# Interleaving two arrays: loads with 63 KiB reads over two SBUF rows

## The chip, the cores and the metric

The kernel runs on one core of a Trainium2 chip. The metric is the device time of one execution in microseconds (us). Before the change the median of three runs is 314.57 us (314.43 to 314.57).

## The reference

```python
def reference(x, y):                       # both (32, 256, 1024) float32
    batch, seq, dim = x.shape
    result = np.zeros((batch, seq, dim * 2), dtype=np.float32)
    result[..., 0::2] = x
    result[..., 1::2] = y
    return result.astype(np.float32)
```

Each input holds 33.55 MB and the output 67.11 MB. No value is changed; elements of x go to the even places of the output and elements of y to the odd ones. Since the last axis is doubled, the whole is also the interleaving of two flat arrays of 8,388,608 elements, and that is how the kernel treats it.

## The kernel before

**Tiles.** The flat arrays are cut into n = 8 tiles of 128 x 8192 elements (W = 8192). A tile's row, one SBUF partition, is 32 KiB and is contiguous in DRAM, and neighbouring partitions hold neighbouring rows of DRAM. There are two buffers each for x (`xt`), y (`yt`) and the woven output (`ot`); `ot` also has 8192 columns, which is the output of half a tile (H = 4096 columns of x and of y). Each half is called a piece here: piece 2k + h is half h of tile k, and it uses `ot[h]`.

**The engines.** Three of them work, and the order of each is written out by hand, with semaphores between them.

- SyncE (SP) issues the loads: the first half of x0 (line 38), then for each tile k x (line 47) and y (line 50). From tile 2 on, x_k waits until the second x copy of tile k-2 is done (line 45), and y_k until the second y copy is (line 49); the semaphore `woven` counts copies. The queue that these loads run on is q1 in the profile.
- VectorE (DVE) weaves: for each piece a copy of x into the even columns of `ot` (line 62) and a copy of y into the odd ones (line 65). It waits for x and y of the tile at its first piece (lines 57 and 64), and before each x copy for the store that last used this `ot` buffer (line 61).
- ScalarE (ACT) issues a small copy from DRAM to DRAM (line 40), the second half of x0 (line 41), and then a store for each piece as soon as its y copy is done (lines 70 to 73). Its queue is q10 in the profile.

**Descriptors.** In a load or store one row of one partition is one descriptor of the DMA engines: 32 KiB for all but the two halves of x0, which have 16 KiB. The 128 rows are shared out over 16 DMA engines, eight for each. A DMA that completes writes a semaphore once on each engine; these are the packets of 4 bytes in the profile's count.

**Start and end.** `tile_interleave_kernel` moves the first DMA of SyncE and of ScalarE ahead of the opening barrier. At the end ScalarE waits for the stores of `ot[0]` and clears semaphores, and SyncE waits for the stores of `ot[1]` (line 79).

Of the kernel before, what the change touches and what calls it, by code (L numbers as in the profile page):

```python
# [3 lines left out]


def _interleave(nc, x, y, out):
    P = 128
    W = 8192
    H = W // 2  # L10

    total = 1
    for s in x.shape:
        total *= s
    n = total // (P * W)
    assert n * P * W == total

    def rows(ap, names, k):
        flat = ap.rearrange("b s d -> (b s d)")
        return flat[k * names : (k + 1) * names].rearrange("(p w) -> p w", p=P)  # L20

    fp32 = mybir.dt.float32
    xt = [nc.alloc_sbuf_tensor(f"xt{b}", [P, W], fp32).ap() for b in (0, 1)]
    yt = [nc.alloc_sbuf_tensor(f"yt{b}", [P, W], fp32).ap() for b in (0, 1)]
    ot = [nc.alloc_sbuf_tensor(f"ot{b}", [P, W], fp32).ap() for b in (0, 1)]

    xsem = [nc.alloc_semaphore(f"xsem{b}") for b in (0, 1)]
    hsem = nc.alloc_semaphore("hsem")
    tsem = nc.alloc_semaphore("tsem")
    ysem = [nc.alloc_semaphore(f"ysem{b}") for b in (0, 1)]  # L30
    woven = nc.alloc_semaphore("woven")
    osem = [nc.alloc_semaphore(f"osem{b}") for b in (0, 1)]

    xs = [rows(x, P * W, k) for k in range(n)]
    ys = [rows(y, P * W, k) for k in range(n)]
    os_ = [rows(out, 2 * P * W, k) for k in range(n)]

    nc.sync.dma_start(out=xt[0][:, :H], in_=xs[0][:, :H]).then_inc(xsem[0], 16)
    few = (slice(0, P, P // 16), slice(0, 128))
    nc.scalar.dma_start(out=os_[0][few], in_=xs[0][few]).then_inc(tsem, 16)  # L40
    nc.scalar.dma_start(out=xt[0][:, H:], in_=xs[0][:, H:]).then_inc(hsem, 16)
    for k in range(n):
        b = k % 2
        if k >= 2:
            nc.sync.wait_ge(woven, 4 * (k - 2) + 3)
        if k:
            nc.sync.dma_start(out=xt[b], in_=xs[k]).then_inc(xsem[b], 16)
        if k >= 2:
            nc.sync.wait_ge(woven, 4 * (k - 2) + 4)
        nc.sync.dma_start(out=yt[b], in_=ys[k]).then_inc(ysem[b], 16)  # L50

    for k in range(n):
        b = k % 2
        for h in (0, 1):
            c = slice(h * H, (h + 1) * H)
            if h == 0:
                nc.vector.wait_ge(xsem[b], 16 * (k // 2 + 1))
            elif k == 0:
                nc.vector.wait_ge(hsem, 16)
            if k:  # L60
                nc.vector.wait_ge(osem[h], 16 * k)
            nc.vector.tensor_copy(out=ot[h][:, 0::2], in_=xt[b][:, c]).then_inc(woven, 1)  # L62
            if h == 0:
                nc.vector.wait_ge(ysem[b], 16 * (k // 2 + 1))
            nc.vector.tensor_copy(out=ot[h][:, 1::2], in_=yt[b][:, c]).then_inc(woven, 1)  # L65

    nc.scalar.wait_ge(tsem, 16)
    for k in range(n):
        for h in (0, 1):
            nc.scalar.wait_ge(woven, 4 * k + 2 * h + 2)  # L70
            nc.scalar.dma_start(
                out=os_[k][:, h * W : (h + 1) * W], in_=ot[h]
            ).then_inc(osem[h], 16)

    nc.scalar.wait_ge(osem[0], 16 * n)
    used = sorted(s.num for s in [*xsem, hsem, tsem, *ysem, woven, osem[0]])
    assert used == list(range(used[0], used[-1] + 1)), used
    nc.scalar.sem_clear(range(used[0], used[-1] + 1))
    nc.sync.nop(nofuse=True).wait_op(osem[1], 16 * n, "sem-ge").then_inc(
        osem[1], -16 * n  # L80
    )


def kernel(tc, x, y, out):
    nc = tc.nc
    tc.close()
    tc.compile()

    _interleave(nc, x, y, out)

    blocks = nc.main_func.blocks
    for engine in (mybir.EngineType.SP, mybir.EngineType.Activation):
        opening = blocks[0].instructions
        at, moved = next(
            (b, i)
            for b in blocks[1:]
            for i in b.instructions
            if i.engine == engine and i.opcode == "DMACopy"
        )
        assert not (moved.sync_info and moved.sync_info.on_wait)  # L100
        body = at.instructions
        body.remove(moved)
        gate = next(
            n
            for n, i in enumerate(opening)
            if i.engine == engine and i.opcode == "Drain"
        )
        opening.insert(gate, moved)
        at.instructions = body
        blocks[0].instructions = opening  # L110


# [1 line left out]
_INS = ['x', 'y']  # L114
_OUTS = [((32, 256, 2048), 'float32')]


# [23 lines left out]
```

## Time and profile before

| what | value |
|---|---|
| median of three runs | 314.57 us |
| span of the profiled execution, first to last instruction | 313.0 us |
| VectorE busy | 72.6 us, 32 copies |
| DMA packets, bytes, mean pace | 4784, 134.23 MB, 429 GB/s |
| q10 (ScalarE's queue): share of 16 engines' span | 51.2% |
| q1 (SyncE's queue): share of 16 engines' span | 48.5% |
| store, issue to landing, median | 29.1 us |
| y load, issue to landing, median | 60.9 us |

The page gives the span of the profiled execution, and no other time of that execution; the median of the timed runs stands 1.57 us above it. Busy shares are taken over the span. The line called DMA cuts the span into 40 slices, and each digit is the mean busy share of the 16 DMA engines in tenths (9 is 90% or more); in a view cut to a window, the slices are those of the window. A line of a queue gives its packets, the megabytes they moved, and the time they took as a share of what 16 engines have in the span. Beside these views the trace holds a record of each DMA packet (queue, size, start and duration); times of single packets in this document come from there. Within one engine a packet starts as soon as the one before it is through, so the records can be strung together by their times, engine by engine.

A line of the timeline gives start and duration in us, the engine, the line of the kernel, the operation with what it writes and reads, and, in brackets, how long the engine was idle before it and what ended that.

### The profile page before, as it was taken

To read this page: it belongs to the slowest core of one execution; us is meant where nothing else is said; L and a number is where in the kernel's file an instruction comes from. 1 tells how busy PE (TensorE), PEld (TensorE's weight loads), DVE (VectorE), ACT (ScalarE), POOL (GpSimd) and SP (SyncE) were. 2 spreads that over 40 slices of the span, in tenths; PEclk is the share of its full clock that TensorE was granted. 3 is DMA by queue.
4 is the path that set the end of the run, shared out by engine and by line. 5 is a ranking of instruction groups with operands and counts; after the bars stand their busy time and mean duration, and the time that the engine had idled before them with its cause. 6 is when DMAs were issued, how large, how long until landed. Compare 5 with 4: busy or idle time off the path is not lost.

```text
span 313.0 us, 115 instructions
## 1 busy us (share of the span) xinstructions
DVE 72.6 (23%) x32; POOL 0.2 (0%) x4
## 2 busy tenths in 40 slices
DVE  0216002231022410325003250031501305013510
POOL 0000000000000000000000000000000000000000
DMA  8999999999999999999999999999999999999998
GB/s 336 435 435 402 465 406 452 419 448 423 435 435 419 452 402 469 402 469 402 465 406 452 419 448 423 435 435 419 452 402 469 402 469 402 465 406 452 419 448 356
DMA packets 4784, 134.23 MB, mean 429 GB/s; under 512 B 544, under 2 KB 560, under 8 KB 560
## 3 DMA queue, kind: packets, MB, share of 16 engines
q10 hardware_dynamic: 2480, 69.22, 51.2%
q1 hardware_dynamic: 2304, 65.01, 48.5%
HBM read 67.12 MB, written 67.12 MB: 429 GB/s over the span
## 4 chain that ended last, share of the span: by engine, by line
DMA 82%; DVE 12%; issue 0%
DMA out_dram<-ot 76%; DVE ot L65 6%; DMA yt<-in_y_dram 6%; DVE ot L62 6%
## 5 line engine op out<-in xcount | busy, mean ns | idle before, releaser
L62 DVE COPY ot<-xt 128x4096 f32<-128x4096 f32 x16 | 36.7, 2295 | 180.2 <-DMA out_dram<-ot 171.5
L65 DVE COPY ot<-yt 128x4096 f32<-128x4096 f32 x16 | 36.7, 2292 | 45.4 <-DMA yt<-in_y_dram 45.4
L125 POOL MEMSET const-bfloat16-1.0<- 128x1 bf16 x1 | 0.1, 101 | 0.0
L125 POOL MEMSET const-uint8-127<- 128x1 uint8 x1 | 0.1, 101 | 0.0
L125 POOL MEMSET const-float32-1.0<- 128x1 f32 x1 | 0.1, 99 | 0.0
L125 POOL MEMSET const-float32-0.0<- 128x1 f32 x1 | 0.1, 98 | 0.2 <-issue 0.2
## 6 DMA issues: line engine op xcount, KB each, us to landing
out_dram<-ot ACTq DMA_DIRECT2D x16, 4096.0 KB, 29.1
yt<-in_y_dram SPq DMA_DIRECT2D x8, 4096.0 KB, 60.9
xt<-in_x_dram SPq DMA_DIRECT2D x7, 4096.0 KB, 43.7
xt<-in_x_dram SPq DMA_DIRECT2D x1, 2048.0 KB, 8.7
xt<-in_x_dram ACTq DMA_DIRECT2D x1, 2048.0 KB, 17.5
out_dram<-in_x_dram ACTq DMA_DIRECT2D x1, 8.0 KB, 6.1
```

The lines of the kernel that those rows point to most:

```text
L62: nc.vector.tensor_copy(out=ot[h][:, 0::2], in_=xt[b][:, c]).then_inc(woven, 1)
L65: nc.vector.tensor_copy(out=ot[h][:, 1::2], in_=yt[b][:, c]).then_inc(woven, 1)
L125: nc = _bacc.Bacc("TRN2", target_bir_lowering=False, num_devices=1)
```

## The change

W becomes 8064, so that a row has 31.5 KiB and two rows have 63 KiB. The 65,536 columns of a partition are then eight tiles of 8064 and a ninth of 1024. Loads, except the two halves of x0, are issued by a new function `load`: the DRAM side is viewed with `fold` neighbouring rows as one (2 for the eight large tiles, 4 for the ninth), the SBUF side stays a tile of 128 rows. A folded load of a large tile so reads 64 pieces of 63 KiB and writes 128 rows of 31.5 KiB; a load of the ninth reads 32 pieces of 16 KiB and writes 128 rows of 4 KiB. The instruction is built by hand from the two access patterns, as the two shapes differ.

The pieces are now a list. The eight large tiles have two pieces of 4032 columns each, the ninth is a single piece of 1024, so there are 17 pieces and 17 stores (16 with rows of 31.5 KiB, one with rows of 8 KiB). Piece i uses `ot[i % 2]`. The waits keep their meaning and are renumbered to the list; the two semaphores of `ot` change their parts in the closing waits, since the last piece now uses `ot[0]`.

```diff
-    W = 8192
-    H = W // 2
+    W = 8064
+    FOLD = 2
...
+    widths = [W] * (cols // W)
+    if cols % W:
+        widths.append(cols % W)
+    n = len(widths)
...
+    pieces = []
+    for k, w in enumerate(widths):
+        step = w // 2 if w > W // 2 else w
+        pieces += [(k, c, c + step) for c in range(0, w, step)]
...
+    def load(tile, ap, k, sem):
+        w = widths[k]
+        fold = FOLD if w == W else 4
+        wide = rows(ap, k).rearrange("(q r) w -> q (r w)", r=fold)
+        return nc.sync.add_instruction(
+            mybir.InstDMACopy(
+                name=nc.get_next_instruction_name(),
+                mode="Copy",
+                engine=mybir.EngineType.SP,
+                queue="qSPDynamicHW",
+                ins=nc.sync.lower_ap_dma(wide),
+                outs=nc.sync.lower_ap_dma(tile[:, :w]),
+            )
+        ).then_inc(sem, 16)
...
         if k >= 2:
-            nc.sync.wait_ge(woven, 4 * (k - 2) + 3)
+            nc.sync.wait_ge(woven, 2 * last[k - 2] + 1)
         if k:
-            nc.sync.dma_start(out=xt[b], in_=xs[k]).then_inc(xsem[b], 16)
+            load(xt[b], fx, k, xsem[b])
         if k >= 2:
-            nc.sync.wait_ge(woven, 4 * (k - 2) + 4)
-        nc.sync.dma_start(out=yt[b], in_=ys[k]).then_inc(ysem[b], 16)
+            nc.sync.wait_ge(woven, 2 * last[k - 2] + 2)
+        load(yt[b], fy, k, ysem[b])
...
+    for i, (k, a, e) in enumerate(pieces):
         b = k % 2
...
+        if i >= 2:
+            nc.vector.wait_ge(osem[i % 2], 16 * (i // 2))
+        o = ot[i % 2][:, : 2 * (e - a)]
+        nc.vector.tensor_copy(out=o[:, 0::2], in_=xt[b][:, a:e]).then_inc(woven, 1)
+        if a == 0:
+            nc.vector.wait_ge(ysem[b], 16 * (k // 2 + 1))
+        nc.vector.tensor_copy(out=o[:, 1::2], in_=yt[b][:, a:e]).then_inc(woven, 1)
...
+    for i, (k, a, e) in enumerate(pieces):
+        nc.scalar.wait_ge(woven, 2 * i + 2)
+        nc.scalar.dma_start(
+            out=rows(fo, k, 2)[:, 2 * a : 2 * e], in_=ot[i % 2][:, : 2 * (e - a)]
+        ).then_inc(osem[i % 2], 16)
...
-    nc.scalar.wait_ge(osem[0], 16 * n)
+    nc.scalar.wait_ge(osem[1 - end], 16 * (m // 2))
...
```

More of the change, by code (lines that the diff above doesn't have):

```diff
@@ L8, in _interleave @@
     P = 128
-    W = 8192
-    H = W // 2
+    W = 8064
+    FOLD = 2
+    fp32 = mybir.dt.float32
     total = 1
@@ L31, in _interleave @@
     woven = nc.alloc_semaphore("woven")
[L32 to L38, printed above, removed]
+    pieces = []
+    for k, w in enumerate(widths):
+        step = w // 2 if w > W // 2 else w
+        pieces += [(k, c, c + step) for c in range(0, w, step)]
+    last = {}
+    for i, (k, _, _) in enumerate(pieces):
+        last[k] = i
+    m = len(pieces)
+    end = (m - 1) % 2
+    osem = [None, None]
+    for b in (1 - end, end):
+        osem[b] = nc.alloc_semaphore(f"osem{b}")
+    def load(tile, ap, k, sem):
[12 more added lines that the diff above has]
+        ).then_inc(sem, 16)
+    H = widths[0] // 2
+    x0 = rows(fx, 0)
+    nc.sync.dma_start(out=xt[0][:, :H], in_=x0[:, :H]).then_inc(xsem[0], 16)
     few = (slice(0, P, P // 16), slice(0, 128))
-    nc.scalar.dma_start(out=os_[0][few], in_=xs[0][few]).then_inc(tsem, 16)
-    nc.scalar.dma_start(out=xt[0][:, H:], in_=xs[0][:, H:]).then_inc(hsem, 16)
+    nc.scalar.dma_start(out=rows(fo, 0, 2)[few], in_=x0[few]).then_inc(tsem, 16)
+    nc.scalar.dma_start(out=xt[0][:, H : widths[0]], in_=x0[:, H:]).then_inc(hsem, 16)
     for k in range(n):
@@ L44, in _interleave @@
         if k >= 2:
-            nc.sync.wait_ge(woven, 4 * (k - 2) + 3)
+            nc.sync.wait_ge(woven, 2 * last[k - 2] + 1)
         if k:
-            nc.sync.dma_start(out=xt[b], in_=xs[k]).then_inc(xsem[b], 16)
+            load(xt[b], fx, k, xsem[b])
         if k >= 2:
-            nc.sync.wait_ge(woven, 4 * (k - 2) + 4)
-        nc.sync.dma_start(out=yt[b], in_=ys[k]).then_inc(ysem[b], 16)
-    for k in range(n):
+            nc.sync.wait_ge(woven, 2 * last[k - 2] + 2)
+        load(yt[b], fy, k, ysem[b])
@@ L53, in _interleave @@
+    for i, (k, a, e) in enumerate(pieces):
         b = k % 2
[L54 to L65, printed above, removed]
@@ L67, in _interleave @@
-    nc.scalar.wait_ge(tsem, 16)
[L68 to L73, printed above, removed]
-    nc.scalar.wait_ge(osem[0], 16 * n)
-    used = sorted(s.num for s in [*xsem, hsem, tsem, *ysem, woven, osem[0]])
+        if a == 0:
+            nc.vector.wait_ge(xsem[b], 16 * (k // 2 + 1))
+        elif k == 0:
+            nc.vector.wait_ge(hsem, 16)
@@ new lines, in _interleave @@
+        if i >= 2:
+            nc.vector.wait_ge(osem[i % 2], 16 * (i // 2))
+        o = ot[i % 2][:, : 2 * (e - a)]
+        nc.vector.tensor_copy(out=o[:, 0::2], in_=xt[b][:, a:e]).then_inc(woven, 1)
+        if a == 0:
+            nc.vector.wait_ge(ysem[b], 16 * (k // 2 + 1))
+        nc.vector.tensor_copy(out=o[:, 1::2], in_=yt[b][:, a:e]).then_inc(woven, 1)
+    nc.scalar.wait_ge(tsem, 16)
+    for i, (k, a, e) in enumerate(pieces):
[3 more added lines that the diff above has]
+        ).then_inc(osem[i % 2], 16)
@@ L77, in _interleave @@
+    nc.scalar.wait_ge(osem[1 - end], 16 * (m // 2))
+    used = sorted(s.num for s in [*xsem, hsem, tsem, *ysem, woven, osem[1 - end]])
     assert used == list(range(used[0], used[-1] + 1)), used
     nc.scalar.sem_clear(range(used[0], used[-1] + 1))
-    nc.sync.nop(nofuse=True).wait_op(osem[1], 16 * n, "sem-ge").then_inc(
-        osem[1], -16 * n
+    turns = (m + 1) // 2
+    nc.sync.nop(nofuse=True).wait_op(osem[end], 16 * turns, "sem-ge").then_inc(
+        osem[end], -16 * turns
     )
```

15 lines of the change are left out of this document (9 added, 6 removed).

## The prediction

> **What bounds the kernel now.** I read the page's busy shares and slices first, then the DMA queues, the DMA view cut to the steady stretch, the waits of the queue that issues loads, and last the order of time at the start and the end.
>
> ```profile
> span 313.0 us, 115 instructions
> DVE 72.6 (23%) x32; POOL 0.2 (0%) x4
> DMA  8999999999999999999999999999999999999998
> DMA packets 4784, 134.23 MB, mean 429 GB/s; under 512 B 544, under 2 KB 560, under 8 KB 560
> q10 hardware_dynamic: 2480, 69.22, 51.2%
> q1 hardware_dynamic: 2304, 65.01, 48.5%
> ```
>
> VectorE works 23% of the span; the 16 DMA engines work 99.7% of it (51.2 + 48.5). q1 is the queue that SyncE issues on (all loads but one), q10 that of ScalarE (all stores, and half of the first load). So the DMA engines bound the kernel, and only three things can move its end: fewer bytes (there are none to save), less cost per descriptor, or stretches in which the engines stall.
>
> ```profile
> DMA  9999999999999999999999999999999999999999
> DMA packets 3661, 106.86 MB, mean 434 GB/s; under 512 B 400, under 2 KB 400, under 8 KB 400
> q1 hardware_dynamic: 1824, 53.48, 50.3%
> q10 hardware_dynamic: 1837, 53.38, 50.3%
> ```
>
> This is the same view from 40 to 286 us. Both queues are always filled and move the same bytes: in the packet records the engines alternate strictly, one load descriptor, one store descriptor. That turns go by descriptor and not by byte is seen before 18 us, where q1 has 32 KiB and q10 has 16 KiB pieces: there too they alternate one to one.
>
> ```profile
> SPq L47 <- DVE ot L62: 208.4, 6, 40.5
> SPq L50 <- DVE ot L65: 11.1, 6, 1.9
> ```
>
> SyncE's queue waits 208.4 us for a copy to free xt. That costs nothing now, because q1 always has about a load in hand: y2 lands at 93.6 us, x3 was issued at 69.64.
>
> ```profile
> 24.24 2.29 DVE L62 COPY ot<-xt 128x4096 f32<-128x4096 f32 x1
> 24.41 274.16 ACTq L71 DMA_DIRECT2D out_dram<-ot  x16
> 26.44 2.29 DVE L65 COPY ot<-yt 128x4096 f32<-128x4096 f32 x1
> ...
> 293.70 2.30 DVE L62 COPY ot<-xt 128x4096 f32<-128x4096 f32 x1 [3.80 <-DMA out_dram<-ot]
> 295.91 2.29 DVE L65 COPY ot<-yt 128x4096 f32<-128x4096 f32 x1
> ```
>
> The first store is issued at 24.41, the last at 298.2 us, while the store ahead of it runs until 302.9: no gap at the end. The one visible stall is at the first store. The load packets that begin at 27.3 to 27.7 us take 1.61 to 1.89 us where all later ones take 1.213, and the first store packets begin at 29.05; with two packets at 26.1 that is 8.8 us over 16 engines, 0.55 us each.
>
> **Prices of descriptors.** From the packet records, start to start on one engine: 1209.5 ns for 32 KiB, 607 for 16 KiB, 23.5 for 512 B, 6 for a semaphore write. Two sizes give the line: (1209.5 - 607)/16384 = 0.036773 ns per byte, and 607 - 602.5 = 4.5 ns for each descriptor (the 512 B one: 18.8 + 4.7, so the line holds). Before, for each engine: 248 x 1209.5 + 16 x 607 + 34 x 6 + 23.5 = 309.9 us. The first packet begins at 1.0, the engines' slow first packets and the stall add 1.7, the last completion falls at 313.0.
>
> **The change, part by part.** Per engine, with the line above.
>
> Stores: 16 x 8 of 31.5 KiB (1190.7 ns) and 8 of 8 KiB (305.7) = 154.86 us, against 128 x 1209.5 = 154.82. More descriptors, +0.04.
>
> First load in two halves of 15.75 KiB: 16 x 597.6 = 9.56, against 9.71 (fewer bytes, which the ninth tile carries).
>
> The 15 folded loads: 60 reads of 63 KiB and 120 writes of 31.5 KiB. No row of before has a read that is split over two writes. If the 4.5 ns go with the read, one costs 2376.8 ns: 142.61 us. If with the write, it costs 2 x 1190.7: 142.88. The ninth tile's two loads: 4 reads of 16 KiB, 2.43, or 16 writes of 4 KiB, 2.48. Before: 120 x 1209.5 = 145.14.
>
> Semaphore writes: 37 instead of 34, +0.02.
>
> Sum: 309.70 us if the read pays, 310.03 if the write pays: -0.20 or +0.13 us. I take -0.20, as the load and the store of 32 KiB cost the same 1209.5 although one writes to SBUF and the other to DRAM, which fits a cost per transfer that the read opens; but that is weak, and +0.13 stays in the range. [...]
>
> VectorE: 34 copies for 32, sixteen pairs of 4032 columns (4032/4096 x 2.29 = 2.25 us) and one of 1024 (0.57). Each pair, 4.5 us, lies under the other buffer's store, which takes 8 x 1.19 = 9.5 us even with the engines to itself. Without that cover each pair would cost up to 4.5 us. The last small pair, 1.1 us, lies under store 15 in the same way. Costed at nothing.
>
> Waits: the counts of woven are renumbered, the order is the same: x of tile k behind the last x copy of tile k-2, y behind the last y copy. Tile 8's loads stand on SyncE behind the copies of piece 13, with two whole stores still to come, and nothing is queued behind them but the closing wait. On ScalarE store 16 stands last, behind store 15. The two longer waits at the end only swap the two semaphores.
>
> Start: y0 now takes 2.38 us turns against 0.60 of the first load's second half. Counting turns from 8.8 us (three of its eight are done): y0 is through at 20.6 instead of 21.5, the half's completion falls at 23.6 instead of 19.1. So the first y copy may begin some 0.9 us earlier and the second x copy about as before. q1 holds x1 and y1 meanwhile, so the engines stay busy and none of this reaches the end.
>
> Turns: if a turn is a read descriptor, q1 gets 63 KiB to q10's 31.5. A tile's loads (8 reads) then take 8 x (2.38 + 1.19) = 28.5 us of a period of some 38, and q1 stands empty for the other 9 or 10, once before each of tiles 3 to 8: six restarts (x2 and y2 still queue up behind y1). With q1 empty, two stores are in hand at 9.5 us each against 4.5 us of copies, so no engine runs out of work. What a restart costs no row shows. The nearest are two of another queue: q10 began again at 6.36 us with a load of 16 KiB pieces beside q1's and cost nothing (neighbours stayed 611 ns), and began again at 29 us with a store, 0.55 us. Mine are loads, so I take nothing, and keep 6 x 0.55 = 3.3 us as the upper end. The first store's own stall I leave at 0.55; it may vanish.
>
> Forecast on the profiled execution: span 313.0 - 0.2 = 312.8. The page gives no time of that execution around its span; the median of the runs lies 1.57 us above it. So 314.57 - 0.2 = 314.4.
>
> **The rivals.** A measurement of this kernel can tell about 0.2% (0.63 us) from no change.
>
> 1. Restarts cost. Place: q1 when SyncE issues x of tiles 3 to 8 into an empty queue. Price: 0.55 us each as at the first store, +3.3 - 0.2: 317.7 us. It decides from 0.14 us a restart (0.83/6). For it: the one restart with 32 KiB pieces stalled all 16 engines. Against it: that was the first store, and the restart by a load was free.
>
> [...]
>
> 3. The descriptors are split again when issued, so that the change does nothing but cut sizes: +0.13, 314.7 us. For it speaks nothing in the trace, which does not hold such a load.
>
> 4. Faster: the first store's stall goes, since a 63 KiB read in hand gives the store time to get ready, and the read pays the 4.5 ns: -0.55 - 0.20, 313.8 us. Against it: no row links the stall to the size of reads.
>
> **How the numbers follow.** My forecast, pace unchanged, 0.33, with its own range 314.2 to 314.7; rival 3, 0.10, also within 0.2%; rival 1, 0.27; rival 2, 0.08; rival 4 and any other saving, 0.22. Faster 0.22, same 0.43, slower 0.35. The predicted time is that of the forecast, 314.4. The range goes down to 313.6 for rival 4 and up to 317.9 for rival 1 with all six restarts at 0.55; rival 2 and a few hundredths beyond the lower end are left out.
>
> **What the profile of the changed kernel would show.** The packet count says who pays: 16 engines x 60 load records if a record is a read, 120 if a write. Turns: from 40 to 286 us q1 should take two thirds of the share while both are filled and fall to nothing for part of each tile; SyncE's wait for xt would stay, but be followed by an empty q1. [...] I am wrong if VectorE's copies come to wait for loads again at tile starts with the engines idle, or if the bytes' pace of 27.2 per ns and engine differs for 63 KiB reads.

## The result, and the profile after

The changed kernel takes 322.44 us (median of four runs, 319.64 to 323.65), the kernel before 314.5 (314.33 to 314.57): a ratio of 1.024, with a 95% interval of 1.020 to 1.028. It is slower by 7.9 us where no change of note was forecast. Its runs lie 1.3% apart, those of the kernel before 0.1%. The profiled run is the fastest of the four, 319.64 us with a span of 318.3.

The page of the changed kernel, the lines that answer to the first fence of the prediction, and the pace in each slice:

```profile
span 318.3 us, 121 instructions
DVE 72.3 (23%) x34; POOL 0.2 (0%) x4
DMA  8998999999999989999999999999999999999995
GB/s 352 460 486 324 454 405 422 413 434 442 434 470 401 446 385 470 389 434 409 422 462 389 438 466 393 450 397 438 442 401 462 418 442 422 430 405 448 434 426 253
DMA packets 4064, 134.23 MB, mean 422 GB/s; under 512 B 592, under 2 KB 608, under 8 KB 608
q10 hardware_dynamic: 2624, 69.18, 50.4%
q1 hardware_dynamic: 1440, 65.05, 48.6%
```

The same bytes take 5.3 us more of span, and the engines still look busy for 99% of it. Two things differ. The last slice holds 253 GB/s instead of 356. And the fourth slice has 324 where it had 402. The packet count answers the question of who pays for a descriptor: q1 has 960 records of 63 KiB, so a record is a read; an undisturbed one lasts 2380 ns and the next begins after 2376 or 2377, 2376.4 on average, within half a nanosecond of the 2372.3 of its bytes by the prediction's line + 4.5. The read pays, once, as taken.

The steady stretch, 40 to 286 us, of the changed kernel:

```profile
DMA  9899999998999999998999998999899999999999
DMA packets 2914, 105.10 MB, mean 427 GB/s; under 512 B 432, under 2 KB 432, under 8 KB 432
q1 hardware_dynamic: 1072, 52.40, 50.4%
q10 hardware_dynamic: 1842, 52.71, 49.7%
```

427 GB/s instead of 434, with 8s among the nines. The engines' time is full by the shares (50.4 + 49.7), so packets last longer than their bytes: of the 960 reads of 63 KiB 799 last 2380 ns to the nanosecond, and 115 that start after 40 us last 50 to 1476 ns more. Summed over engines and divided by 16, load packets after 40 us are 3.0 us too long and store packets 0.2. Before the change there is not one such packet after 40 us.

The turns are as forecast, two bytes of load to one of store. From 90 to 116 us, with both queues filled, q1 moves 7.23 MB to q10's 3.74:

```profile
DMA packets 260, 10.97 MB, mean 422 GB/s; under 512 B 32, under 2 KB 32, under 8 KB 32
q1 hardware_dynamic: 128, 7.23, 65.3%
q10 hardware_dynamic: 132, 3.74, 33.3%
```

The load queue runs dry, as forecast too. From 79.5 to 88 us, in the changed kernel:

```profile
DMA packets 126, 3.74 MB, mean 440 GB/s; under 512 B 10, under 2 KB 10, under 8 KB 10
q10 hardware_dynamic: 121, 3.74, 102.0%
q1 hardware_dynamic: 5, 0.00, 0.0%
```

q1 moves nothing there, and stores alone fill the engines. The long packets come right after it. From 126 to 134 us:

```profile
DMA packets 76, 3.32 MB, mean 415 GB/s; under 512 B 12, under 2 KB 12, under 8 KB 12
q1 hardware_dynamic: 39, 2.52, 84.0%
q10 hardware_dynamic: 37, 0.81, 23.5%
```

q1 moves 2.52 MB in 84% of the engines' time; at 2380 ns a read it would need 73%. This is the first load of tile 4, and one engine's packets there read 2380, 2892, 2736, 2380 ns where another's read 2380, 3856. The end shows what that does. First the kernel before, from 308 to 313 us, then the changed one from 313 us on:

```profile
DMA  0000699960000099990000009999000000000000
DMA packets 64, 1.57 MB, mean 315 GB/s; under 512 B 16, under 2 KB 16, under 8 KB 16
```

```profile
DMA  9777959978722324252421222141212211100000
DMA packets 126, 0.96 MB, mean 182 GB/s; under 512 B 23, under 2 KB 23, under 8 KB 23
q10 hardware_dynamic: 126, 0.96, 43.1%
```

Before, all 16 engines begin their packets together and stop together. (A packet counts in the slice where it starts, so the gaps between the 9s are not idle time.) After, the share falls slowly from 9 to 1: the engines are no longer in step. With the records strung together engine by engine, their last packets end between 314.3 and 317.9 us, on average at 315.6; before, between 312.2 and 312.7, on average at 312.4. Every engine moves the same bytes (8.39 of the 134.23 MB), and the last one sets the end.

So the 5.3 us of span are: 3.2 us by which the mean engine is later (0.2 saved on descriptors, 3.2 lost in long packets after 40 us, 0.3 at the first store, whose stall is 0.85 instead of 0.55; 0.1 is left over), and 2.1 us more by which the slowest engine is behind the mean than before (2.3 against 0.2). This is the account of the profiled run alone, the fastest of the four; the others were not profiled.

### The profile page after: what moved, and what is told of

Its sections match the earlier page's. It is cut to its first block, busy times and chain, and to the rows that moved or that the text cites. A ratio compares the mean times of both kernels' runs of the same rounds, so it can differ in the third digit from the quotient of the medians.

```text
span 318.3 us, 121 instructions
## 1 busy us (share of the span) xinstructions
DVE 72.3 (23%) x34; POOL 0.2 (0%) x4
## 2 busy tenths in 40 slices
DMA packets 4064, 134.23 MB, mean 422 GB/s; under 512 B 592, under 2 KB 608, under 8 KB 608
## 3 DMA queue, kind: packets, MB, share of 16 engines
q10 hardware_dynamic: 2624, 69.18, 50.4%
## 4 chain that ended last, share of the span: by engine, by line
DMA 85%; DVE 11%; issue 0%; DVEq 0%; ACTq 0%
DMA out_dram<-ot 79%; DMA yt<-in_y_dram 6%; DVE ot L99 6%; DVE ot L96 5%; DVEq L94 0%; ACTq L103 0%
## 5 line engine op out<-in xcount | busy, mean ns | idle before, releaser
L96 DVE COPY ot<-xt 128x4032 f32<-128x4032 f32 (+1 forms) x17 | 36.9, 2169 | 225.2 <-DMA out_dram<-ot 215.7
L99 DVE COPY ot<-yt 128x4032 f32<-128x4032 f32 (+1 forms) x17 | 36.8, 2163 | 10.3 <-DMA yt<-in_y_dram 10.3
```

What stands on the lines that cost most here:

```text
L96: nc.vector.tensor_copy(out=o[:, 0::2], in_=xt[b][:, a:e]).then_inc(woven, 1)
L99: nc.vector.tensor_copy(out=o[:, 1::2], in_=yt[b][:, a:e]).then_inc(woven, 1)
```

## The experiments

The three theories that the first runs were to part: A, uneven turns make the load queue run dry, and the restarts stall (the prediction's first rival); B, the length of a 63 KiB read; C, the fold, one read spread over several writes. The "descriptor sum" of a run is the prediction's sum for one engine, redone for that run's sizes. "Long packets" below are the sum of what load packets after 40 us last over their size's time, over 16 engines; 0.0 in the kernel before.

**Loads unfolded, all else as changed.**

```diff
-        fold = FOLD if w == W else 4
+        fold = 1
```

> The changed kernel with every load unfolded (a read for each row: 31.5 KiB for the large tiles, 4 KiB for the ninth); tiles, pieces, stores and waits as changed. By all three theories below the slowdown goes: 60 more reads per engine at 4.5 ns on the 309.7 us of the changed kernel's sum, 314.7 us. If it stays at 319 or more, the cause is the sizes or the ninth tile and not the folded read.

315.29 us, 1.0022 of before (1.0013 to 1.0032). Long packets 0.0; the engines finish between 312.5 and 313.2. The view from 40 to 286 us:

```profile
DMA  9999999999999999999999999999999999999999
DMA packets 3749, 106.55 MB, mean 433 GB/s; under 512 B 416, under 2 KB 416, under 8 KB 450
```

All nines, 433 GB/s. The tiles of 8064, the ninth tile and the instruction built by hand (its issue takes SyncE 0.47 us instead of 0.33) cost only the descriptors, with some 0.3 us more at the first store. Folding the loads brings the loss. The edit also makes reads shorter and turns even, so the next runs take these apart.

**Two to one turns without a fold.** The kernel before, each store in two DMAs of half rows.

```diff
-            nc.scalar.dma_start(
-                out=os_[k][:, h * W : (h + 1) * W], in_=ot[h]
-            ).then_inc(osem[h], 16)
+            for c in (0, H):
+                nc.scalar.dma_start(
+                    out=os_[k][:, h * W + c : h * W + c + H], in_=ot[h][:, c : c + H]
+                ).then_inc(osem[h], 16)
```

> The kernel before, with each store cut into two DMAs of 16 KiB rows; loads stay unfolded at 32 KiB. Turns then go two bytes of load to one of store, as in the changed kernel, with no fold and no read over 32 KiB. Theory A (uneven turns make the load queue run dry and the engines stall where loads come in again): six to seven stalls of 0.3 to 0.9 us mean as in the changed kernel, and engines out of step, 317 to 322 us. Theories B (the length of a 63 KiB read) and C (one read spread over several writes): only 128 more descriptors per engine and 16 more semaphore writes, +0.7 us, 315.2 us.

315.15 us, 1.0020 (1.0011 to 1.0030), what the descriptors cost. From 77.5 to 85 us, and then from 40 to 286 us:

```profile
DMA packets 214, 3.19 MB, mean 426 GB/s; under 512 B 19, under 2 KB 19, under 8 KB 19
q10 hardware_dynamic: 214, 3.19, 99.4%
```

```profile
DMA  9999999999999999999999999999999999999999
DMA packets 5500, 106.11 MB, mean 431 GB/s; under 512 B 624, under 2 KB 624, under 8 KB 624
```

No line of q1 stands in the first view at all: the load queue runs dry here in the same way, once a tile, and starts again. Yet all slices are nines, long packets are 0.0, and the engines finish within 0.4 us of each other. Theory A falls as it stood: a restart of unfolded 32 KiB loads beside half-row stores costs nothing.

**Folded reads at even turns.** Tiles of 4032 columns in four buffers, a piece is a whole tile.

```diff
-    W = 8064
-    FOLD = 2
+    W = 4032
+    LOAD_FOLD = 2
+    B = 4
...
-    xt = [nc.alloc_sbuf_tensor(f"xt{b}", [P, W], fp32).ap() for b in (0, 1)]
+    xt = [nc.alloc_sbuf_tensor(f"xt{b}", [P, W], fp32).ap() for b in range(B)]
...
-            nc.sync.wait_ge(woven, 2 * last[k - 2] + 1)
+            nc.sync.wait_ge(woven, 2 * (k - B) + 1)
...
```

> Tiles of 4032 columns, four buffers each for x and y, a piece is a whole tile. Each load read is 31.5 KiB and is written as two rows of 15.75 KiB; stores have 31.5 KiB rows. So reads are folded, but a load's turn is as long as a store's. Theory A: even turns, no dry load queue, about as before, 314.3 to 315.2 us. Theory B: the same. Theory C: as slow as the changed kernel, 318 to 323 us.

323.67 us, 1.031 (1.027 to 1.035). At the end most engines idle from some 302 to 309 us, because the last large tile's y lands late on a few of them (up to 305.7 us) and the last stores wait for its copies. That wait is itself a consequence of the stalls: the latest engine, strung together, has some 8 us of long packets and is never idle before 308 us, while the mean engine has 2.5 us of them and idles for 5.7. So with equal turns and a load queue that never runs dry, long packets are 2.1 us (and 0.5 in stores), where the unfolded 31.5 KiB reads of the first run have none. B alone can't do this. No unfolded kernel in tiles of 4032 columns was run, though, so what the narrow tiles add by themselves, here and in the two later kernels that use them, isn't shown.

**Four rows a read, 63 KiB, in tiles of 4032 columns.** (`LOAD_FOLD = 4` in the kernel above.)

> As the kernel with tiles of 4032 columns, but each load read takes four rows, 63 KiB. Turns are two to one again. Theory A: loads run dry several times and stall, 317 to 323 us; with the finer waits (SyncE may issue 2 MiB at a time) there are more restarts, twice as many, each for half the bytes. Theory B: 317 to 323 us as well, since the reads are 63 KiB. Theory C: slow, and worse than with two rows a read.

318.47 us, 1.0145 (1.010 to 1.019); long packets 1.3 us, engines' ends from 313.3 to 315.9. Theories A, B and C all expected a loss; it is smaller than with two rows, against what C expected.

**The loads' order.** y ahead of x.

```diff
         if k >= 2:
-            nc.sync.wait_ge(woven, 2 * last[k - 2] + 1)
-        if k:
-            load(xt[b], fx, k, xsem[b])
-        if k >= 2:
             nc.sync.wait_ge(woven, 2 * last[k - 2] + 2)
         load(yt[b], fy, k, ysem[b])
+        if k:
+            load(xt[b], fx, k, xsem[b])
```

> The changed kernel with SyncE issuing y of a tile ahead of x, both behind the last y copy of the tile two before. In the changed kernel nearly all long load packets were in x loads from tile 2 on (3.0 of 3.3 us a mean engine, of which tiles 2, 4 and 6 took 2.0) and almost none in y loads. Theory P (the place: a folded load that starts soon after the load queue ran dry and a new store began): the long packets move to the y loads, x loads are clean, 318 to 323 us. Theory Q (the array: x's addresses against the output's): the long packets stay in x loads, 318 to 323 us. If neither load has them, the slowdown goes: 314.3 us.

323.45 us, 1.028 (1.025 to 1.030). The long packets move to the y loads, which now come first in their tile (some 4.5 of 5.3 us; stores have another 1.6 us). So it is the place: the first load of a tile, not the array or its addresses.

**Only x folded, and only y folded.**

```diff
-        fold = FOLD if w == W else 4
+        fold = 1 if ap is fy else FOLD if w == W else 4
```

> The changed kernel with x loads folded (63 KiB reads) and y loads unfolded (31.5 KiB reads). Theories P and Q: the stalls stand in the x loads that are still folded: 317 to 323 us. Theory R (each folded read may stall, wherever it stands, and y was spared by chance): half of the loss, 316.5 to 319 us.

322.37 us, 1.027 (1.023 to 1.030), as much as with both. Of its 2.9 us of long packets 0.4 are not folded reads: from 69 to 76 us, 24 unfolded y reads of tile 2 last 50 to 510 ns too long, and no engine has a folded read under way meanwhile.

```diff
-        fold = FOLD if w == W else 4
+        fold = 1 if ap is fx else FOLD if w == W else 4
```

> The changed kernel with y loads folded and x loads unfolded. Theories P and Q: x loads stand in the bad place but are unfolded, y loads are folded but stand in a good place: no stalls but the one at the first store, 314.5 us. Theory R: half of the loss, 316.5 to 319 us.

316.29 us, 1.0064 (1.0047 to 1.0081); long packets 0.7 us. The loss is nearly all there when the first load of a tile is folded, and little of it when only the second is, so P holds with a rest that it doesn't explain. More than half of that rest (0.37 us) lies in 17 x reads, unfolded ones, of tiles 5 and 6, again with no folded read under way. So a kernel with folded loads stalls, but it is not only the folded reads that last too long.

**The changed kernel again**, for the next three runs.

> The changed kernel once more, on the chip of the next three: 319.5 to 324 us. Its second profile shows whether the long load packets fall to the same tiles again (2, 4 and 6 most) or to others.

320.87 us, 1.022 (1.018 to 1.025). Long packets 3.5 us, engines' ends from 315.3 to 319.0. They stand in the first loads of tiles 2 to 7 again, and most in tile 4 again, but tiles 5 and 7 now have three times what they had (0.57 and 0.65 us for 0.21 and 0.18): the place repeats, the amounts don't.

**First loads later, clear of the store's beginning.**

```diff
             nc.sync.wait_ge(woven, 2 * last[k - 2] + 1)
+            nc.sync.wait_ge(osem[0], 16 * (k - 1))
```

> The changed kernel; before x of tile k SyncE also waits until the first store of tile k-2 is through, so that the folded x load starts some 5 us after the next store has begun, and no store begins in its first 9 us. The load queue is dry for longer, with a store of 9.5 us in hand. If the stalls need a store that begins while a folded load runs its first packets, they go: 314.3 to 315.5 us. If a folded load that starts into a dry queue is enough, they stay: 318 to 324 us. If the engines now run out of work, it shows as idle slices and not as long packets.

319.62 us, 1.016 (1.0145 to 1.0175). Tiles 3 and 4 lose their long packets; tiles 2, 5, 6 and 7 keep or gain them (2.9 us in all). A store that begins at the same time isn't needed.

**Quarter pieces in four output buffers**, folded, and the same unfolded.

```diff
-        step = w // 2 if w > W // 2 else w
+        step = w // 4 if w > W // 2 else w
...
-        if i >= 2:
-            nc.vector.wait_ge(osem[i % 2], 16 * (i // 2))
+        if i >= 4:
+            nc.vector.wait_ge(osem[i % 4], 16 * (i // 4))
```

> The changed kernel with pieces of a quarter tile (2016 columns, store rows of 15.75 KiB) and four output buffers instead of two halves, so that two to three stores are always queued and none begins soon after it was issued. Turns are four to one in bytes. If the stalls come from a store that was issued only some 5 us before its turn, they go: sum 309.7 + 0.7 for the added store descriptors and semaphore writes, 315.2 us. If not, 318 to 324 us.

> The quarter pieces with unfolded loads (31.5 KiB reads, turns two to one): by every theory no stalls but the first store's, 315.6 us. It is what the folded one is to be compared with.

Folded 317.12 us, 1.0099 (1.0066 to 1.0132); unfolded 315.85, 1.0044 (1.0029 to 1.0059). Long packets 0.3 and 0.1 us. Most of the stall is gone, with reads of 63 KiB and a dry queue in every tile, but 1.3 us remain between the two, more than the descriptors give (the folded one has 0.3 us fewer).

**Two against three output buffers**, W = 7168, so that three fit.

```diff
-    W = 8064
+    W = 7168
+    B = 3
...
-        if i >= 2:
-            nc.vector.wait_ge(osem[i % 2], 16 * (i // 2))
+        if i >= B:
+            nc.vector.wait_ge(osem[i % B], 16 * (i // B))
```

> The changed kernel with W = 7168 (nine tiles and a tenth of 1024 columns; folded reads of 56 KiB, store rows of 28 KiB), two output buffers as now. It is the comparison for the next run. By the descriptor sum 309.8 us for each engine, 314.3 without stalls; I expect the stalls, 318 to 323 us.

> The same with three output buffers, so that a store is issued a whole store's time (8.5 us alone) earlier before its turn, while the load queue still runs dry and starts again in each tile, with reads twice as long as stores. If the stalls come from a store that is issued only some 5 us before its turn while a folded load starts, they go: 314.3 to 315.5 us. If the folded load that starts into a dry queue is enough, they stay: 318 to 323 us.

321.85 us (1.024, 1.022 to 1.026) and 321.88 (1.022, 1.019 to 1.026). With the third buffer the profiled run's long packets fall from 4.5 to 1.3 us, but not the time. Its tail from 312 us on says why:

```profile
DMA  9869434373010300020000200000000000000000
DMA packets 104, 0.81 MB, mean 90 GB/s; under 512 B 20, under 2 KB 20, under 8 KB 20
q10 hardware_dynamic: 104, 0.81, 21.3%
```

After some 315 us nearly every slice is 0 to 3: 14 engines are done by 315, one at 315.7, and a single one works until 320.6. That engine has 7.2 us of long packets, loads and stores together, where the mean engine has 1.4; the end waits for it alone.

**Unfolded reads of 63 KiB.** Tiles of 16128 columns with one buffer each for x and y; `fold = 1`. A tile's loads wait for the last copies of the tile before.

> Unfolded reads of 63 KiB: tiles of 16128 columns, one buffer each for x and y, four pieces a tile, stores of 31.5 KiB rows as in the changed kernel. The single buffers leave the engines idle at every tile, so the time says nothing (340 us or more); what counts are the load packets. If the length of the read makes the stalls, 63 KiB loads beside starting stores show packets 0.3 to 1.5 us too long, as in the changed kernel. If the fold does, they show none but at the first store.

338.88 us in one run, by its single buffers. After the first dry time, here of some 31 us, the first load packet is 0.9 to 1.9 us too long on all 16 engines, and the store packet ahead of it 0.3 to 1.1: 1.96 us a mean engine. The next two restarts of wide loads are alike; the last one, of the narrow closing tile, has no long load packet. So an unfolded load can stall too, and I did not expect that. Unlike in the changed kernel all engines stall alike and stay in step; they end between 337.0 and 337.1.

Theory D in the following texts is that a load read and a store row have to fit together: they are harmless as long as their two lengths together stay small enough. By the runs above, 63 + 15.75 KiB would fit (long packets 0.3 us with quarter pieces), 56 + 28 and 63 + 31.5 would not (4.5 us with W = 7168, 3.0 us in the changed kernel); that is the author's estimate from these runs, and none of them shows what would set such a limit.

**The same with reads of half the length, and with store rows of half the length.**

```diff
-        wide = rows(ap, k).rearrange("(q r) w -> q (r w)", r=fold)
...
+        for c in range(0, w, w // 2):
+            nc.sync.dma_start(
+                out=tile[:, c : c + w // 2], in_=rows(ap, k)[:, c : c + w // 2]
+            ).then_inc(sem, 16)
```

> The kernel of unfolded 63 KiB reads with each load cut into two DMAs of 31.5 KiB reads; the same single buffers, dry load queue and waits, so the time is again 335 us or more. In the run with 63 KiB the first load packet after each dry time was 1.0 to 1.8 us too long on all 16 engines, and the store packet ahead of it 0.3 to 1.1 us. If the length of the read does that, both go (under 0.3 us). If a long dry time does it, they stay.

```diff
-        step = w // 4 if w > W // 2 else w
+        step = w // 8 if w > W // 2 else w
```

> The kernel of unfolded 63 KiB reads with pieces half as large: store rows of 15.75 KiB, two output buffers of 15.75 KiB. Theory D: the long packets at the restarts go, since 63 + 15.75 KiB fit. If the length of the read alone does it, they stay at 1.0 to 1.8 us. The time says nothing.

337.85 and 335.34 us, one run each. At the first restart 1.1 us are lost with 31.5 KiB reads (and 0.3 at the second DMA), 1.1 with 63 KiB reads beside store rows of 15.75 KiB, against 1.96. Half-length reads don't take it away, so in these kernels about 1.1 us comes with the restart, and a long read beside a long store row comes with 0.9 more. Neither expectation held outright, and each figure is of a single run.

**Do read and store row have to fit together?** W = 6144: 48 KiB reads, 24 KiB store rows.

```diff
-    W = 8064
+    W = 6144
...
-        fold = FOLD if w == W else 4
+        fold = FOLD
```

> The changed kernel with W = 6144 (ten tiles and an eleventh of 4096 columns, all loads folded by two): reads of 48 KiB, store rows of 24 KiB, two output buffers, turns two to one, the load queue dry in each tile as before. [...] Theory C (the fold): 318 to 322 us.

325.69 us as the median of five runs (322.63 to 330.58), 1.036 (1.034 to 1.038), the slowest of the double-buffered ones; long packets 4.4 us in the profiled run, the fastest of the five, and engines idle for another 2.2 us. By theory D 48 + 24 KiB would have to fit, with no stalls but the first store's. Theory D falls.

**The harmless sizes, folded.** Tiles of 4032 columns, half pieces in four output buffers: reads of 31.5 KiB over two rows, store rows of 15.75 KiB.

```diff
-        step = w // 2 if w > W // 2 else w
+        step = w // 2 if w == W else w
...
-        wide = rows(ap, k).rearrange("(q r) w -> q (r w)", r=fold)
+        wide = folded(ap, k, 1, LOAD_FOLD if w == W else 4)
```

> Folded reads of 31.5 KiB (two rows of 15.75 KiB) beside store rows of 15.75 KiB in four output buffers: the sizes and turns of the half-row stores of the kernel before, with folded in place of unfolded reads. Sum 310.7 us for each engine: 315.4 us if the fold alone costs nothing at this size (theory D). Theory C: 317 us or more, with long load packets in many tiles.

318.51 us, 1.0133 (1.0109 to 1.0157), 3.1 us over its descriptor sum. Long packets are 1.1 us, and 0.5 in stores; the engines end between 313.8 and 316.4. The page of this run:

```profile
span 316.8 us, 192 instructions
DMA  9999999999999999999999999999999999999997
DMA packets 7569, 134.24 MB, mean 424 GB/s; under 512 B 1088, under 2 KB 1104, under 8 KB 1104
```

The kernel with half-row stores has nearly the same sizes (32 and 16 KiB) and the same turns without a fold, and loses nothing. Closer still are the unfolded quarter pieces, with the same 31.5 KiB reads, 15.75 KiB store rows and four output buffers: 315.85 us, long packets 0.1. At sizes and turns that are harmless unfolded, then, the folded kernel is 2.7 us slower; what else differs is the narrow tile with its four buffers for x and y, which was not run unfolded.

## Why the prediction was wrong

**The step that failed** is the cost of the folded reads: they were costed at the pace of the unfolded ones, plus or minus a descriptor ("pace unchanged", 0.33). Their price per descriptor was right within half a nanosecond, 2376.4 against 2376.8. But load packets then stall at certain places, 3.0 us a mean engine in the changed kernel's profile, where its twin with unfolded loads has 0.0. The sum had no term for that, and none for engines that fall out of step, which put the slowest another 2.1 us later.

**What held.** The read pays the 4.5 ns. Turns go by read, two to one (7.23 to 3.74 MB from 90 to 116 us). q1 runs dry before each of tiles 3 to 8, for 7.8 to 8.9 us without a load packet on any engine, and stores alone fill the engines meanwhile (102.0% from 79.5 to 88 us). The first y copy began 0.8 us earlier (21.24 for 22.03), the second x copy as before (24.22 for 24.24), and neither reached the end. VectorE's copies stayed hidden, and after the first tile none waited for a load.

**Rival 1, restarts.** Its price of 3.3 us is close to the 3.2 by which the mean engine was later in the profiled run, which is luck, since the price came from one stall of another kind; and its place is nearly right: first loads of a tile. Its cause is not: half-row stores give the same dry times and restarts for nothing, tile 2's first load stalled although its queue wasn't dry (0.57 us between 52 and 58 us), and the even-turn kernel stalls without dry times. What the half-row kernel lacked was the fold. I had looked for the price of a restart among unfolded loads, and beside half-row stores it was free there as the trace said; the error was to carry that to a load of another kind.

**What no rival had** is that the stalls fall unevenly on the engines. The sum, and the upper end 317.9 with all six restarts at 0.55 us, were made for one engine that stands for all 16, because in the trace of before they finish within 0.5 us. After, the slowest sets the end, 2.3 us behind the mean in the profiled run and 6.5 us in the run with three output buffers. By the mean engine's 3.2 us alone 314.5 would have become 317.7, just inside the range; in the profiled run the slowest engine put it outside, at 319.64. How the further 2.8 us of the median, 322.44, divide between the two isn't known.

**Rival 2**, loads at a far lower pace throughout (a chance of 0.08), is out, and no run shows a term for it. From 8.2 to 20 us, with no stores beside them, all 64 folded 63 KiB reads of y last 2380 ns, as the undisturbed ones later do, on all engines. A slower pace that begins only once the engines are out of step was not tested. **Rival 3** is out by the 960 records of 63 KiB. **Rival 4**: the first store's stall did not go, it grew from 0.55 to 0.85 us; it also grew with unfolded loads of 31.5 KiB (0.86) and with half-row stores (0.73), so it has little to do with the fold.

**What stays open** is why a kernel with folded loads stalls. Shown: every folded variant that I ran is slower than its descriptor sum, by 1.8 us at the least (y folded alone), and the unfolded ones with double buffers are within 0.7 us of theirs; the first load of a tile carries most, where that was looked at; small store rows in four buffers reduce it. Not needed: uneven turns, a dry queue, 63 KiB, or a store that begins at the same time. Nor need the packet that stalls be a folded read, or any folded read be under way: 0.4 us of long packets in each of the two half-folded kernels are unfolded reads. So the fold brings the stalls, but they can't be a price of the folded read alone. Whether a folded load gives the engines other rows than an unfolded one can't be seen, since the records carry no rows. Stores folded in the same way, which would make turns of 63 KiB on both sides, were not tried.

No variant came under the kernel before. What the fold can save by the packet records is the 4.5 ns of each descriptor, 0.3 us in 60 reads an engine.

## What to carry to other kernels

A sum per engine gave the end of this DMA-bound kernel as long as the 16 engines stayed in step: before, they end within 0.5 us of each other; after, the slowest ends 2.3 us behind the mean. So look at the slope of the DMA share in the last microseconds: in the run with three output buffers a single engine works until 320.6 us where 14 are done by 315, which the mean engine's 1.4 us of long packets doesn't show. The price taken from unfolded reads held for the folded ones (2376.4 ns for 2376.8), but it says nothing of the stalls, 0.0 us a mean engine with unfolded loads and 3.0 with folded ones. Where a change brings a load that the trace has never shown, a small fixed saving stands against a stall of unknown size, and the range has to say so. And merging the 32 KiB descriptors of these loads could win only a few tenths of a microsecond in 314, 60 times 4.5 ns.

## What was unexpected in the hardware

- The turn between the two queues is one read descriptor, at unlike sizes too: in the kernel before, from 8 to 18 us, 95 descriptors of 32 KiB on q1 (3.11 MB) stand against 90 of 16 KiB on q10 (1.47 MB); in the changed one, from 90 to 116 us, 112 of 63 KiB against 116 of 31.5 KiB.
- Engines that got out of step did not always find back: in these kernels the early ones wait for the late one only by way of the copies, once a piece. In the run with three output buffers the mean engine idles 0.1 us after 40 us, and at the end one engine is still at work at 320.6 us where 14 were done between 312.5 and 314.9. With W = 6144 they do wait, 2.2 us, and 15 of them end within 0.3 us.
- Run to run, the changed kernel scatters by 1.3% (319.64 to 323.65 us), while the kernel before and the unfolded ones with double buffers repeat within 0.3%.
- A restart of unfolded loads cost 1.1 to 2.0 us a mean engine in the single-buffered kernels, after 31 to 37 us without a load, and nothing in the kernel with half-row stores, where q1 moves nothing from 77.5 to 85 us. No run says whether the length of the dry time makes the difference.
